# Eight pairs of row blocks by seven products in place of nine, in a feed-forward layer on one Trainium2 core

## The chip, the cores and the metric

The kernel runs on one core of a Trainium2 chip. Times are microseconds (us) of device time for one execution. The engines are named as the profile names them: PE is TensorE (matmuls; PEld its weight loads), DVE is VectorE, ACT is ScalarE, POOL is GpSimd, and SP is SyncE, which issues most of the DMA loads.

## The reference

The kernel computes a small decoder trunk: 256 tokens, 1,024 model columns (D), two layers, all in float32. Each layer is an attention (a different one per layer), a SwiGLU feed-forward of 2,816 features, and a gated embedding of 256 columns ("ple"); one RMS norm closes it. Cut to what matters here:

```python
for i in range(DEPTH):                      # 2 layers
    h = h + attention_i(rmsnorm(h))         # left out
    u = rmsnorm(h, ffn_norm_g[i])
    gu = u @ ffn_w_in[i]                    # 1024 -> 2 * 2816
    h = h + (silu(gu[..., :D_FF]) * gu[..., D_FF:]) @ ffn_w_out[i]
    gate = sigmoid(rmsnorm(h, ple_norm_g[i]) @ ple_w_gate[i])
    h = h + gate * (p[i] @ ple_w_up[i])
return rmsnorm(h, final_norm_g)
```

The change lies in the product with `ffn_w_out`, in the order of the steps around it, and in one small step of the last "ple".

## The kernel before, in words

**Numbers.** A float32 matrix is split into a high and a low part of the matmul's reduced type: ScalarE copies it (rounded) and VectorE subtracts the copy (`split`, L322 and L323, and the same inside `half`, L188 and L189, or, in pieces, L164 and L169). A product is then three matmuls, high by high, high by low and low by high (`mm3`, L100 to L102). The running sum h is held with the columns on the partitions (`hx`, printed as `gx`): eight blocks of 128 columns by 256 tokens. Its first four blocks are called half 0, the others half 1.

**Weights.** All weights lie in one array in the order of their use, 216 blocks of 128 by 1,024 values (512 KB). `half` and `blocks` take the next block: SP loads it into one of six `raw` buffers, ScalarE and VectorE split it into one of six `whi` and six `wlo` buffers. A block normally feeds 24 matmuls of 256 columns or 12 of 512. For some blocks a form is named, which splits the block in two pieces, a first block of 128 columns and the rest, or lays them apart; the constant `AGAIN` names the feature blocks, `(4, 0)` to `(20, 0)` by twos, that are split with their first eighth by itself (`_BOTH1`).

**The feed-forward (`ffn`).** The 2,816 features are 22 blocks of 128 (FT = 22), taken in eleven pairs, f = 0, 2, ... 20. For one feature block `up` makes gate and up projection, 48 matmuls into one PSUM bank (`gu`). `gated` then scales it (VectorE L631, which reads the bank), takes Silu (ScalarE L638), multiplies (VectorE L639) and splits the result into `fh` and `fl`, which are `prod[f]`. PSUM has eight banks, and each bank has one user at a time: a matmul that begins a new use waits until the old one has been read.

The product with `ffn_w_out` is made pair by pair, and its two output halves in two ways:

- Half 1 is made directly: `down(f)` takes one weight block and runs 24 matmuls (`feature_unit`) into the two banks `acc[1]` (`fo`).
- Half 0 is made for the first nine pairs (f < SEVEN = 18) by seven products in place of eight (`products`): the pair is a 2 by 2 matrix of blocks (two feature blocks by two halves of 256 output columns) times a 2 by 2 matrix (two feature blocks by two halves of 128 tokens). Seven products of three matmuls, 21, replace 24; they go into the four banks `seven` (`fs`), with tokens on the partitions. For this VectorE makes sums of the weight block (`sevenfold`, L198 to L200, `sums`) and differences of the gated features (`differences`, L651 to L653, `dif`), and both engines split the sums, the differences and the block itself.
- For the other two pairs (f = 18 and 20) half 0 is made directly, by `last(f, 0)`: 24 matmuls into `acc[0]`. `last(f, 1)` does half 1 of these pairs at the end.

**Order.** The loop at L704 runs, for each f, `up([f])`, `up([f + 1])`, then `down(f - 2)` for the pair before. At f = 16 `filler()` loads p and splits it. After `down(16)`, at f = 18, `combined` (L668) adds the four banks `fs` into a tile c: one ScalarE copy (L672, `m`) and five VectorE additions (L674 to L679). Then come `up([20])` and `up([21])`. After the loop: `last(18, 0)`; `turned(c)` (L682), which turns c back by eight transposes on TensorE (L687) into two banks `fc` and adds these to half 0 of hx (`residual`, VectorE L349, two instructions); `filler(pp)`, which is `ple_up`, the product of p with `ple_w_up` into four banks (`pu`); `last(20, 0)`; a second `residual` for half 0; `last(18, 1)`, `last(20, 1)`, and the `residual` of half 1. At `filler(pp)` four of the eight banks are held by `acc[0]` and `acc[1]`, so that `pu` needs the other four.

**Who sets the order.** A planner walks through the program ahead of the run with estimated times and fixes for each engine, and for SP's queue, one order of its instructions; it prefers what stands earlier in the program, among what its estimate says is ready. Each engine then runs its list in that order and waits where an input or a buffer isn't free. `tc.high_priority()` moves the instructions inside it ahead in the planner's preference. `tc.issue_after(x)` puts those instructions inside it that run on x's engine behind x.

**The last "ple" (layer 1).** In `ple` (L808 on), gate products in two halves are followed by the final norm. A third weight tile u (the last 256 columns of `ple_w_up`) is loaded (L871) and split (L873) into `uhi` and `ulo`; its product `pu_own` is the last work of TensorE. L868 multiplies the first half of h by the final norm's gains, one instruction for each half of the tokens (`end`). The buffers of u have the tag `qkt`, of which there are four; the split differences `dh` and `dl` of a pair take two of these.

Of the kernel before, what the change touches and what calls it, by code (L numbers as in the profile page):

```python
# [13 lines left out]
ALU = mybir.AluOpType  # L14
# [7 lines left out]
NP = H // 2  # L22
DFF = 2816
FT = DFF // P
SEVEN = FT - 4
DP = 256
EPS = 1e-6
BUCKETS = 32
# [3 lines left out]
HC = 512  # L32
# [41 lines left out]
    ((2, 8), (0, 0), 0), ((0, 0), (2, 8), 64)  # L74
FORMS = {(_l, 0, _j): _HI2 for _l in range(2) for _j in (0, 4, 6)}
FORMS.update({(_l, "wo", _n): _HI2 for _l in range(2) for _n in (0, 2, 4)})
AGAIN = tuple((f, 0) for f in range(4, FT, 2))

# [1 line left out]
def trunk(ctx: ExitStack, tc: tile.TileContext, pt, w, cst, gf, out):  # L82
    nc = tc.nc
# [6 lines left out]
    def bank(name):  # L90
        return ps.tile([P, 512], F32, tag="bank", name=name)

    def f32(ap):
        return ap.bitcast(F32)
# [3 lines left out]
    def mm3(o, a, b, start, stop):  # L98
        (ah, al), (bh, bl) = a, b
        mm(o, ah, bh, start=start, stop=False, skip_group_check=True)  # L100
        mm(o, ah, bl, start=False, stop=False, skip_group_check=True)  # L101
        return mm(o, al, bh, start=False, stop=stop, skip_group_check=True).ins  # L102
# [108 lines left out]
    def blocks(entry=False, form=None):  # L211

        if form:
            return half(APART, 0, form)
        hi, lo = half(APART, ENTRY * P if entry else 0)
        hi = [hi[:, k * P:(k + 1) * P] for k in range(KT)]
        return hi, lo if entry else [lo[:, k * P:(k + 1) * P] for k in range(KT)]
# [103 lines left out]
    def split(hi, lo, src):  # L321
        nc.scalar.activation(hi, src, AF.Copy)  # L322
        nc.vector.tensor_tensor(lo, src, f32(hi), op=ALU.subtract)  # L323
# [15 lines left out]
    def feature_unit(bks, wt, off, x, start, stop):  # L339

        hi, lo = wt
        for m in range(4):
            o = bks[m // 2][:, (m % 2) * S:(m % 2 + 1) * S]
            mm3(o, (hi[off + m], lo[off + m]), x, start and m % 2 == 0, stop)

    def residual(hf, bks):
        for b in range(2):
            at = hx[:, 4 * hf + 2 * b:4 * hf + 2 * b + 2].rearrange("p m s -> p (m s)")
            nc.vector.tensor_tensor(at, at, bks[b], op=ALU.add)  # L349
# [240 lines left out]
    def ffn(layer, nm, filler, np_):  # L590
# [3 lines left out]
        def up(fs):  # L594
# [25 lines left out]
            for a in range(2):  # L620
                wt = blocks(form=_BOTH1 if (fs[0], a) in AGAIN else None)
                for k in range(KT):
# [5 lines left out]
        def gated(fs, bks):  # L628
            for f in fs:
                t = work.tile([P, 2, S], F32, tag="t2k", bufs=3, name=f"gut{layer}_{f}")  # L630
                nc.vector.tensor_tensor(t, bks[f].rearrange("p (a s) -> p a s", s=S), nm.rows(), op=ALU.mult)  # L631
                if f >= SEVEN:
                    sg = work.tile([P, S], F32, tag="sg", name=f"sg{layer}_{f}")
# [9 lines left out]
                prod[f] = th, tl  # L643
                if f < SEVEN and f % 2:
                    differences(f // 2)

        def differences(i):

            q = quarters.pop(i).rearrange("p k (t s) -> p (k t) s", s=P)
            d = work.tile([P, 4, P], F32, tag="tt", bufs=3, name=f"dif{layer}_{i}")  # L650
            nc.vector.tensor_tensor(d[:, 0:2], q[:, 2:3].to_broadcast([P, 2, P]), q[:, 0:4:3], op=ALU.subtract)  # L651
            nc.vector.tensor_tensor(d[:, 2], q[:, 3], d[:, 0], op=ALU.subtract)
            nc.vector.tensor_tensor(d[:, 3], q[:, 1], d[:, 2], op=ALU.subtract)  # L653
            dh, dl = [work.tile([P, 4, P], F32R, tag="qkt", bufs=4, name=f"d{x}{layer}_{i}") for x in "hl"]
            split(dh, dl, d)
            diff[i] = dh, dl

        def products(i):

            b11, b22, b21, x1, x2, x3, x4 = sevenfold()  # L660
            (a11, a21), (_, a22) = [[[x[:, t * P:(t + 1) * P] for x in prod[2 * i + k]] for t in range(2)] for k in range(2)]
            a3, a7, a1, a6 = [[x[:, n] for x in diff[i]] for n in range(4)]
            m43, m1, m52, m76 = seven
            for o, at, new, a, b in ((m43, 0, 1, a22, b21), (m52, 1, 1, a21, b11), (m43, 1, 0, a3, b22), (m52, 0, 0, a11, x2),
                                     (m1, 0, 1, a1, x3), (m76, 1, 1, a6, x1), (m76, 0, 0, a7, x4)):
                mm3(o[:, at * S:(at + 1) * S], a, b, bool(new) and i == 0, i == SEVEN // 2 - 1)

        def combined():  # L668

            m43, m1, m52, m76 = [b.rearrange("p (a s) -> p a s", s=S) for b in seven]  # L670
            m = work.tile([P, 2, S], F32, tag="t2k", bufs=3, name=f"m43_{layer}")
            nc.scalar.activation(m, m43, AF.Copy)  # L672
            c = work.tile([P, 4, S], F32, tag="bias", bufs=1, name=f"c{layer}")
            nc.vector.tensor_tensor(c[:, 2], m[:, 0], m52[:, 1], op=ALU.add)  # L674
            nc.vector.tensor_tensor(c[:, 1], m[:, 1], m52[:, 0], op=ALU.add)
            o = c[:, 0:4:3]
            nc.vector.tensor_tensor(o, m, m52, op=ALU.subtract)
            nc.vector.tensor_tensor(o, o, m1[:, 0:1].to_broadcast([P, 2, S]), op=ALU.add)
            nc.vector.tensor_tensor(o, o, m76, op=ALU.add)  # L679
            return c.rearrange("p (t n) s -> p t (n s)", n=2)  # L680

        def turned(c):  # L682

            bks = [bank(f"fc{layer}_{b}") for b in range(2)]
            for m in range(4):
                for t in range(2):
                    nc.tensor.transpose(bks[m // 2][:, (m % 2) * S + t * P:(m % 2) * S + (t + 1) * P],  # L687
                                        c[:, t, m * P:(m + 1) * P], ident)
            residual(0, bks)

        def down(f):
            wt = blocks()
            for i in range(2):
                feature_unit(acc[1], wt, 4 * i, prod[f + i], f + i == 0, False)
            products(f // 2)

        def last(f, hf):

            wt = blocks(form={(FT - 2, 0): _BOTH1, (FT - 2, 1): _BOTH1}.get((f, hf)) if layer else None)
            for i in range(2):  # L700
                feature_unit(acc[hf], wt, 4 * i, prod[f + i], hf == 0 and f + i == SEVEN, f + i == FT - 1)

        early = up([0, 1])
        for f in range(2, FT, 2):  # L704
            up([f])
            up([f + 1])
            if layer == 0 and f in (6, 8, 10, 12):
                moba[0](f // 2 - 3)
            if f == FT - 6:
                pp = filler()  # L710
            if f == 2:
                seven.extend(bank(f"fs{layer}_{t}") for t in range(4))
                acc[1] = [bank(f"fo{layer}_1_{t}") for t in range(2)]
            if f < FT - 2:
                down(f - 2)
            if f == SEVEN:
                c = combined()
        acc[0] = [bank(f"fo{layer}_0_{t}") for t in range(2)]
        last(FT - 4, 0)
        turned(c)  # L720
        filler(pp)
        last(FT - 2, 0)
        residual(0, acc[0])
        last(FT - 4, 1)
        np_.turn(0)
        if layer == 0:
# [103 lines left out]
    def ple(layer, nm, ut, nx):  # L830
        if layer == 0:
            return ple_first(nm, ut, nx)
        h = token["h"]
# [8 lines left out]
        bks = [[bank(f"pg{layer}_{hf}_{t}") for t in range(2)] for hf in range(2)]  # L842
# [9 lines left out]
        gb, ys = end[:, 2], end[:, 0:2]  # L852
# [5 lines left out]
        def square(t, i, c0, c1):  # L858

            sq = work.tile([P, S], F32, tag="sg", name=f"sqf{t}_{i}") if i else \  # L860
                work.tile([P, HC], F32, tag="t2k", bufs=3, name=f"sqf{t}_{i}")
            nc.scalar.activation(sq[:, 0:c1 - c0], h[:, t, c0:c1], AF.Square, scale=D ** -0.5,
                                 accum_out=ss[:, t, i:i + 1])

        for t in range(2):
            square(t, 0, 0, HC)
            nc.vector.tensor_scalar(ms[:, t, 0:1], ss[:, t, 0:1], EPS, None, op0=ALU.add)
            nc.vector.tensor_tensor(ys[:, t, 0:HC], h[:, t, 0:HC], gb[:, 0:HC], op=ALU.mult)  # L868
        wts = [half(3 * APART) for _ in range(4)]
        uraw, uhi, ulo = [work.tile([P, 2, S], F32R if i else F32, tag="qkt", bufs=4, name=f"u{i}") for i in range(3)]  # L870
        nc.sync.dma_start(uraw, bass.AP(tensor=w.tensor, offset=w.offset + w_at(UP) + HC + S,  # L871
                                        ap=[[HW, P], [P * HW, 2], [1, S]]))
        split(uhi, ulo, uraw)  # L873
        uown = bank("pu1_own")
        own = bank(f"pg{layer}_own")

# [76 lines left out]
def _wide(a, c, hf):  # L953

    t = a[c * P:(c + 2) * P, hf * HC:(hf + 1) * HC]
    return t.reshape(2, P, HC).transpose(1, 0, 2).reshape(P, HW)


def _quarters(a, c):

    t = a[c * P:(c + 2) * P, 0:HC].reshape(2, P, 2, S)
    return np.concatenate([t[0, :, 1], t[0, :, 0], t[1, :, 1], t[1, :, 0]], 1)
# [80 lines left out]
```

## Time and profile before

| what | us |
|---|---|
| median of 3 runs | 643.4 (642.76 to 644.86) |
| the profiled execution, its own time | 641.55 |
| its span, from the first to the last instruction | 639.6 |
| TensorE busy | 630.3 (99% of the span) |
| VectorE busy | 522.6 (82%) |
| ScalarE busy | 404.9 (63%) |
| DMA traffic | 125.20 MB, mean 196 GB/s |
| granted TensorE clock | 0.998 |

The profile is one execution. A line of a group names the source line, the engine, the operation, the tile written and the tiles read (`out<-in`), the shapes, the count, then busy time, mean nanoseconds of one, and the idle time of the engine ahead of it with what ended it. A line of the timeline has the start and the length in us; a bracket at its end names idle time ahead of it and what ended that. In the list of waits stand the sum, the number of times and the longest. Matmul records have a modelled end and overlap each other: a 256-column matmul's record is 0.28 us long, though the next one starts well before that, so that the distance of starts is the better measure.

### The profile page before, as it was taken

The numbers are of one execution on the slowest core, as the hardware profiler recorded it, in microseconds if no ns is written. First come the engines' busy times: TensorE is split into PE (matmuls) and PEld (weight loads), VectorE is DVE, ScalarE is ACT, GpSimd is POOL, SyncE is SP. The second block draws the span as 40 slices with busy tenths as digits, with TensorE's granted clock in tenths as the row PEclk, the third lists the DMA queues.
The fourth block names the chain that finished last, engine by engine and source line by source line (L and its number), as shares of the span: only waits on it lengthen the run. The fifth ranks groups of instructions, "written<-read, shape, count | busy, mean of one in ns | idle before, by whom it ended". The sixth has DMA issues, their size and how long they took to land.

```text
span 639.6 us, 13330 instructions
## 1 busy us (share of the span) xinstructions
PE 630.3 (99%) x5262; PEld 608.3 (95%) x5262; DVE 522.6 (82%) x988; ACT 404.9 (63%) x737; POOL 16.3 (3%) x33
## 2 busy tenths in 40 slices
PE   9999999999999999999999999999999999999996
PEld 7899999999999999999989999999999999999885
DVE  6987985899888788889997787588988887888865
ACT  7857675766555455758875586558555555545772
POOL 2500000000000000000000000000000000000002
PEclk9999999999999999999999999999999999999999
DMA  8889744267555556776687544325666666557701
GB/s 328 303 269 372 230 152 146 78 198 230 188 191 184 182 191 205 251 232 194 201 283 246 180 150 133 132 76 188 200 198 199 198 198 198 191 200 228 239 2 66
DMA packets 37214, 125.20 MB, mean 196 GB/s; under 512 B 3968, under 2 KB 7072, under 8 KB 37152
## 3 DMA queue, kind: packets, MB, share of 16 engines
q1 hardware_dynamic: 36832, 123.91, 58.5%
q8 instruction: 41, 0.67, 0.4%
q10 hardware_dynamic: 320, 0.44, 0.2%
q14 instruction: 21, 0.17, 0.1%
HBM read 123.25 MB, written 4.24 MB: 199 GB/s over the span
## 4 chain that ended last, share of the span: by engine, by line
PE 91%; DVE 4%; issue 2%; ACT 2%; POOL 0%; POOLq 0%; DVEq 0%; ACTq 0%
PE gu L100 11%; PE gu L102 11%; PE gu L101 11%; PE pq L100 5%; PE pq L101 5%; PE pq L102 5%; PE fo L100 3%; PE fo L102 3%; PE fo L101 3%; PE wo L100 2%; PE wo L102 2%; PE wo L101 2%; PE fs L102 2%; PE fs L100 2%; PE fs L101 2%
## 5 line engine op out<-in xcount | busy, mean ns | idle before, releaser
L189 DVE TENSOR_TENSOR wlo<-raw,whi 128x1024 fp32r<-128x1024 f32 (+1 forms) x166 | 197.5, 1195 | 28.4 <-ACT whi L188 28.2
L188 ACT ACTIVATE whi<-raw 128x1024 fp32r<-128x1024 f32 (+1 forms) x166 | 169.1, 1032 | 59.1 <-issue 20.8
L100 PE MATMUL gu<-g,whi 128*128 128x256 f32 x702 | 194.0, 276 | 0.0
L102 PE MATMUL gu<-g,wlo 128*128 128x256 f32 x702 | 194.0, 276 | 0.0
L101 PE MATMUL gu<-g,whi 128*128 128x256 f32 x702 | 193.9, 276 | 0.0
L102 PEld LDWEIGHTS gu<-g,wlo 128*128 128x128 f32 x702 | 131.9, 188 | 0.0
L100 PEld LDWEIGHTS gu<-g,whi 128*128 128x128 f32 x702 | 131.8, 188 | 0.0
L101 PEld LDWEIGHTS gu<-g,whi 128*128 128x128 f32 x702 | 131.8, 188 | 0.0
L100 PE MATMUL pq<-g,whi 128*128 128x256 f32 x256 | 71.1, 278 | 0.0
L102 PE MATMUL pq<-g,wlo 128*128 128x256 f32 x256 | 70.8, 276 | 0.0
L101 PE MATMUL pq<-g,whi 128*128 128x256 f32 x256 | 70.7, 276 | 0.0
L164 ACT ACTIVATE whi<-raw 128x128 fp32r<-128x128 f32 (+1 forms) x72 | 41.8, 622 | 27.8 <-PE pq L101 6.6
L100 PE MATMUL fo<-fh,whi 128*128 128x256 f32 x208 | 57.5, 277 | 0.0
L102 PE MATMUL fo<-fh,wlo 128*128 128x256 f32 x208 | 57.5, 276 | 0.0
L101 PE MATMUL fo<-fl,whi 128*128 128x256 f32 x208 | 57.4, 276 | 0.0
L169 DVE TENSOR_TENSOR wlo<-raw,whi 128x128 fp32r<-128x128 f32 (+1 forms) x72 | 48.1, 686 | 10.4 <-ACT whi L164 10.3
L100 PEld LDWEIGHTS pq<-g,whi 128*128 128x128 f32 x256 | 48.1, 188 | 1.1 <-issue 0.7
L101 PEld LDWEIGHTS pq<-g,whi 128*128 128x128 f32 x256 | 48.1, 188 | 0.1
L102 PEld LDWEIGHTS pq<-g,wlo 128*128 128x128 f32 x256 | 48.1, 188 | 0.0
L638 ACT ACTIVATE tt<-gut 128x256 f32<-128x256 f32 x36 | 14.9, 413 | 44.1 <-DVE gut L631 44.1
L198 DVE TENSOR_TENSOR sums<-raw 128x512 f32<-128x512 f32 x18 | 12.4, 690 | 35.1 <-DMA raw<-w 35.1
L101 PEld LDWEIGHTS fo<-fl,whi 128*128 128x128 f32 x208 | 39.1, 188 | 0.0
(216 smaller groups left out, 1359.1 us busy)
## 6 DMA issues: line engine op xcount, KB each, us to landing
raw<-w SPq DMA_DIRECT2D x212, 512.0 KB, 4.2
d<-d SPq DMA_DIRECT2D x4, 768.0 KB, 9.1
raw<-w SPq DMA_DIRECT2D x8, 256.0 KB, 5.0
bias<-d SPq DMA_DIRECT2D x4, 512.0 KB, 7.8
bias<-cd SPq DMA_DIRECT2D x2, 768.0 KB, 8.1
gx<-w SPq DMA_DIRECT2D x1, 512.0 KB, 5.1
bias<-cd SPq DMA_DIRECT2D x1, 512.0 KB, 7.8
p<-pt SPq DMA_DIRECT2D x2, 256.0 KB, 4.1
```

What stands on the lines that cost most here:

```text
L100: mm(o, ah, bh, start=start, stop=False, skip_group_check=True)
L101: mm(o, ah, bl, start=False, stop=False, skip_group_check=True)
L102: return mm(o, al, bh, start=False, stop=stop, skip_group_check=True).ins
L164: nc.scalar.activation(o, raw[:, c], AF.Copy)
L169: nc.vector.tensor_tensor(t[:, a + b0 * P:a + b1 * P], raw[:, b0 * P:b1 * P], f32(ht[:, a0:a0 + (b1 - b0) * P]), op=ALU.subtract)
L188: nc.scalar.activation(hi[:, c], raw[:, c], AF.Copy)
L189: nc.vector.tensor_tensor(lo[:, c], raw[:, c], f32(hi[:, c]), op=ALU.subtract)
L198: nc.vector.tensor_tensor(more[:, 0:2], raw[:, 1:3], raw[:, 0:1].to_broadcast([P, 2, S]), op=ALU.add)
L638: nc.scalar.activation(sg, t[:, 0], AF.Silu)
```

## The change

`SEVEN` becomes FT - 6 = 16. Pair f = 16 leaves the seven products: it has no sums, differences or products, and `last(16, 0)` makes its half 0 directly, ahead of `last(18, 0)`. `combined` comes at f = 16, after `down(14)`. `turned(c)` moves from after the loop to f = 18, after `down(16)` and ahead of `up([20])`, and its `residual` gets the high priority. `AGAIN` ends at `(18, 0)`, so that the first block of `up([20])` is split in one piece. In `ple`, the split of u is placed inside `issue_after` of the second instruction of L868. The order of the weight array follows: the block of pair 16 for half 0 stands as an ordinary block behind those of `up([21])` instead of as a block of quarters.

```diff
-SEVEN = FT - 4
+SEVEN = FT - 6
-AGAIN = tuple((f, 0) for f in range(4, FT, 2))
+AGAIN = tuple((f, 0) for f in range(4, SEVEN + 4, 2))
...
         def turned(c):
-            residual(0, bks)
+            with tc.high_priority():
+                residual(0, bks)
 
         def down(f):
             wt = blocks()
             for i in range(2):
                 feature_unit(acc[1], wt, 4 * i, prod[f + i], f + i == 0, False)
-            products(f // 2)
+            if f < SEVEN:
+                products(f // 2)
 
-        def last(f, hf):
+        def last(f, hf, mid=None):
             wt = blocks(form={(FT - 2, 0): _BOTH1, (FT - 2, 1): _BOTH1}.get((f, hf)) if layer else None)
             for i in range(2):
+                if i and mid:
+                    mid()
                 feature_unit(acc[hf], wt, 4 * i, prod[f + i], hf == 0 and f + i == SEVEN, f + i == FT - 1)
...
             if f == SEVEN:
                 c = combined()
+            if f == SEVEN + 2:
+                turned(c)
         acc[0] = [bank(f"fo{layer}_0_{t}") for t in range(2)]
+        last(SEVEN, 0)
         last(FT - 4, 0)
-        turned(c)
         filler(pp)
         last(FT - 2, 0)
...
-            nc.vector.tensor_tensor(ys[:, t, 0:HC], h[:, t, 0:HC], gb[:, 0:HC], op=ALU.mult)
+            begun = nc.vector.tensor_tensor(ys[:, t, 0:HC], h[:, t, 0:HC], gb[:, 0:HC], op=ALU.mult).ins
...
-        split(uhi, ulo, uraw)
+        with tc.issue_after(begun):
+            split(uhi, ulo, uraw)
...
             if f < FT - 2:
-                seq += [_wide(fout[i], f - 2, 1), _quarters(fout[i], f - 2)]
-        seq.append(_wide(fout[i], FT - 4, 0))
+                seq += [_wide(fout[i], f - 2, 1)] + [_quarters(fout[i], f - 2)] * (f <= SEVEN)
+        seq += [_wide(fout[i], f, 0) for f in (SEVEN, FT - 4)]
```

The new parameter `mid` of `last` has no caller that uses it.

## The prediction

> **What bounds the kernel.** I read the page first: busy times, granted clock, and the engines' shares of the chain that ended last.
>
> ```profile
> PE 630.3 (99%) x5262; PEld 608.3 (95%) x5262; DVE 522.6 (82%) x988; ACT 404.9 (63%) x737; POOL 16.3 (3%) x33
> PEclk9999999999999999999999999999999999999999
> PE 91%; DVE 4%; issue 2%; ACT 2%; POOL 0%; POOLq 0%; DVEq 0%; ACTq 0%
> ```
>
> TensorE is the bound, at full clock throughout. Work taken from VectorE or ScalarE is worth nothing by itself; only fewer matmuls, or a wait of TensorE that ends, shorten the run. So the next view is the list of TensorE's waits, here in full:
>
> ```profile
> PE pu L100 <- DVE gx L349: 2.1, 2, 1.4
> PE cold L133 <- PEq L1035: 0.8, 1, 0.8
> PE pu L100 <- DVE gut L631: 0.2, 1, 0.2
> ```
>
> Apart from the start, TensorE waits only in `pu`, the filler, twice for the additions at L349 (the `residual` of `turned`) and once for the reader of a `gu` bank at L631. Matmul records overlap, so this list understates the loss. The timeline of starts shows it, layer 0 first, then layer 1:
>
> ```profile
> 284.36 0.28 PE L101 MATMUL pu<-plo,whi 128*128 128x256 f32 x1
> 284.47 0.28 PE L102 MATMUL pu<-phi,wlo 128*128 128x256 f32 x1
> 285.41 0.38 PE L100 MATMUL pu<-phi,whi 128*128 128x256 f32 x1 [0.66 <-DVE gx L349]
> 285.63 0.28 PE L101 MATMUL pu<-plo,whi 128*128 128x256 f32 x1
> ...
> 594.43 0.39 PE L101 MATMUL pu<-wlo,phi 128*128 128x512 f32 x1
> 594.66 0.40 PE L102 MATMUL pu<-whi,plo 128*128 128x512 f32 x1
> 595.25 0.50 PE L100 MATMUL pu<-whi,phi 128*128 128x512 f32 x1 [0.19 <-DVE gut L631]
> 595.58 0.40 PE L101 MATMUL pu<-wlo,phi 128*128 128x512 f32 x1
> ...
> 596.51 0.39 PE L102 MATMUL pu<-whi,plo 128*128 128x512 f32 x1
> 598.29 0.50 PE L100 MATMUL pu<-whi,phi 128*128 128x512 f32 x1 [1.39 <-DVE gx L349]
> 598.62 0.40 PE L101 MATMUL pu<-wlo,phi 128*128 128x512 f32 x1
> ```
>
> Undisturbed, starts follow each other by 0.11 us for 256 columns (284.36 to 284.47) and 0.23 for 512 (594.43 to 594.66). The first matmul after a wait also takes one extra step, so I count two steps each time. Layer 0: 284.47 to 285.63 is 1.16, less 0.22: 0.94 lost. Layer 1: 0.92 less 0.46 is 0.46, and 2.11 less 0.46 is 1.65. Together 3.05 us. Why VectorE is late shows in its own timeline, with the transposes on TensorE between:
>
> ```profile
> 284.68 1.28 DVE L349 TENSOR_TENSOR gx<-gx,fc 128x512 f32<-128x512 f32 x2
> ...
> 590.91 0.68 DVE L323 TENSOR_TENSOR u<-u,u 128x512 fp32r<-128x512 f32 x1
> 592.63 1.04 PE L687 MATMUL fc<-cs,c 128*128 128x128 f32 x8
> 594.51 0.69 DVE L631 TENSOR_TENSOR gut<-gu,row 128x512 f32<-128x512 f32 x1
> ...
> 597.55 1.28 DVE L349 TENSOR_TENSOR gx<-gx,fc 128x512 f32<-128x512 f32 x2
> ```
>
> The eight transposes end at 593.7, but VectorE still works through the last two features, weight splits and u, and adds only at 597.55. The filler needs four banks; two of them hold the transposes until these additions have read them. The bank read by L631 at 594.51 holds feature 21, and the `pu` matmul of 595.25 starts as that read ends. So the loss is one of order: VectorE's queue reaches the two additions about 4 us after their input is there.
>
> **The change, part by part.** *Ninth pair direct.* A direct half and a seven-product stage stand side by side:
>
> ```profile
> 262.21 0.28 PE L100 MATMUL fo<-fh,whi 128*128 128x256 f32 x1
> 264.93 0.28 PE L100 MATMUL fs<-whi,fh 128*128 128x256 f32 x1
> 267.35 0.28 PE L100 MATMUL gu<-g,whi 128*128 128x256 f32 x1
> ```
>
> 24 matmuls take 2.72 us, 21 take 2.42: +0.30 per layer, +0.60 in two, all on the bound engine, hidden by nothing. Bounds: two steps of 0.11 (0.44 in all) to three whole records of 0.28 (1.68); I take the measured stages, as they are the same instructions on the same tiles.
>
> [...]
>
> *What VectorE is spared.* Sums of weights, differences and their splits go, one plain split comes:
>
> ```profile
> L189 DVE TENSOR_TENSOR wlo<-raw,whi 128x1024 fp32r<-128x1024 f32 (+1 forms) x166 | 197.5, 1195 | 28.4 <-ACT whi L188 28.2
> L198 DVE TENSOR_TENSOR sums<-raw 128x512 f32<-128x512 f32 x18 | 12.4, 690 | 35.1 <-DMA raw<-w 35.1
> L323 DVE TENSOR_TENSOR wlo<-sums,whi 128x1024 fp32r<-128x1024 f32 x18 | 22.0, 1220 | 1.8 <-ACT whi L322 1.8
> ```
>
> 0.69 + 1.22 - 1.20 is at least 0.7 us per layer off VectorE, besides the smaller sums, the quarter block's split and the differences. On the end this is worth 0, since VectorE is not the bound; it is lead for what follows. The number of weight loads stays: a wide block comes where the quarter block was. Only the second raw buffer that a seven-product pair takes for its sums is no longer asked for, so SyncE's loads can run earlier, not later.
>
> *Sums a pair sooner.* `combined` (one ScalarE copy, five VectorE additions) moves ahead of `up(18)`, `up(19)` and `down(16)` in program order; the transposes move ahead of `up(20)`, `up(21)` and the direct stages. If c is not there when TensorE reaches them, everything behind them waits in TensorE's order, `up(20)` first.
>
> ```profile
> 562.84 0.28 PE L102 MATMUL fs<-whi,dl 128*128 128x256 f32 x1
> 576.58 0.28 PE L100 MATMUL fs<-whi,fh 128*128 128x256 f32 x1
> 578.88 0.28 PE L102 MATMUL fs<-whi,dl 128*128 128x256 f32 x1
> 588.38 0.68 DVE L679 TENSOR_TENSOR c<-c,fs 128x512 f32<-128x512 f32 x1
> ```
>
> Today c is finished at 589.06, 10.2 us after the last product (578.88). The transposes will stand where pair nine's products stood, 13.7 us after pair eight's (562.84 to 576.58). 3.5 us to spare, so I take 0. It can't be below nothing, as no wait for c is in the list now; upward it starts only when c slips by more than 3.5. The stretch itself has less in it than pair nine's had, by the pieces above. The eight transposes move and are not added.
>
> *Additions first.* From the transposes to `pu` lie two features and, newly, two direct stages:
>
> ```profile
> 579.00 0.28 PE L100 MATMUL gu<-g,whi 128*128 128x256 f32 x1
> 589.79 0.28 PE L102 MATMUL gu<-g,wlo 128*128 128x256 f32 x1
> ```
>
> 10.8 + 2 x 2.72 = 16.2 us for additions of 1.28, so their wait goes whole. What is late next is the bank of `up(21)`: its reader ended at 595.20, 5.4 us after the last `gu` matmul (589.79), and the two direct stages put `pu` 5.5 us after it. Even on today's timetable that just fits, and VectorE has lost c's additions and u's 0.68 from this stretch against 1.28 that come. So the 0.46 goes too.
>
> *`(20, 0)` in one piece; u later.* Rows for the lead of weights, and for u:
>
> ```profile
> 578.38 1.23 DVE L189 TENSOR_TENSOR wlo<-raw,whi 128x1024 fp32r<-128x1024 f32 x1 [0.53 <-ACT whi L188]
> 581.74 0.28 PE L100 MATMUL gu<-g,whi 128*128 128x256 f32 x1
> ...
> 573.80 0.63 ACT L322 ACTIVATE u<-u 128x512 fp32r<-128x512 f32 x1 [1.90 <-DMA u<-w]
> ...
> 627.70 0.79 DVE L839 TENSOR_TENSOR pgt<-pgt,ut 128x256 f32<-128x256 f32 x2 [2.10 <-ACT pgt L838]
> ```
>
> A block's low part is ready at 579.61 and used at 581.74: a lead of 2.1 us, the shortest near the end of the loop. The form that `(20, 0)` loses splits its first eighth ahead of the rest, so that TensorE could begin on it sooner; whole, the block is ready at most one split (1.20) later for its first matmul, inside the lead: 0. If that lead were gone, up to 0.9 per layer. Of the u split only VectorE's half is bound, behind the second addition of L868, since `issue_after` binds what runs on the engine of the instruction that it names. It then falls into the 2.10 us that VectorE stands idle before 627.70, and 0.68 fits: 0. If it lands behind 627.70 it lies on the way to the end: +0.68. Its reader, the last `pu_own` matmuls, comes later still. ScalarE's copy, with its 1.90 us wait for the load of u, stays free to come early; in before it lies ahead of pair ten's splits and costs TensorE nothing.
>
> **Sum:** -0.94 - 0.46 - 1.65 + 0.60 = -2.45 us. The profiled execution took 641.55 (span 639.6, 1.95 around it), so 639.1; on the runs' median, 643.4, it is 640.95, say 641.0, or -0.38%. The 1.85 us by which that median lies above the profiled execution I leave as it is, since nothing in the change bears on it.
>
> **The rivals.**
> *Slower: VectorE stands at the additions.* Put first in its order, they could be reached before the transposes are done. Then VectorE waits, and behind it the splits of the blocks for `up(20)` and `up(21)`, for which TensorE waits next.
>
> ```profile
> DVE sums L198 <- DMA raw<-w: 35.1, 12, 4.4
> ```
>
> VectorE does stand like that, up to 4.4 us for one load. The lead of 2.1 absorbs part; from a stand of 2.1 + 1.2 = 3.3 us per layer on, the gain is gone. A stand of 5.5 costs 3.4 per layer, 6.8 less 2.45: 647.8. Against it: VectorE runs behind TensorE here (feature 21 read 4.7 us after its matmuls), so it will come late, not early. [...]
>
> *c comes late.* `filler` loads p just ahead of pair eight's products; if ScalarE's copy of m43 goes behind the split of p and that load is late, c slips. Waiting starts at 3.5 us of slip; at 4.5 in both layers 2.0 come back: 643.0, no change.
>
> *The gu bank instead.* If VectorE reads feature 21 some 0.6 us later against TensorE than now, `pu` waits 0.5 in each layer: -1.45, 642.0, just no change. For it: 5.4 against 5.5 us is no margin by itself. Against it: what VectorE has lost from that stretch.
>
> *u's copy on ScalarE a pair sooner.* Its buffers come free a pair earlier, so its 1.90 us wait may fall among pair eight's splits; doubled, it outruns the lead by 1.7 in layer 1: -0.75, 642.7, no change.
>
> *Not what it says:* the order alone could clear the wait and the priority do nothing. Then the additions would come behind feature 21 again, but with 16.2 us instead of none between transposes and `pu` they are still in time: the forecast's 641.0, and no chance of its own.
>
> **How the numbers follow.** About 0.3% (1.9 us) is what a measurement of this kernel can tell from no change; the forecast is half a microsecond beyond it. Forecast 0.70, of which the runs' scatter and the 0.44 to 1.68 of the added matmuls put 0.13 within 0.3%; VectorE standing 0.06 (slower); c late 0.07 and u 0.07 (no change, 0.01 each slower); gu bank 0.10 (0.07 no change). That makes faster 0.60, same 0.32, slower 0.08. The range, 640.1 to 643.0, reaches below to the lower bound of the added matmuls (640.8) and the runs' scatter, above to the rivals without a change; the slower rival and the tails, some 0.15, are left out.
>
> **What would show it.** Right: no TensorE wait for gx in `pu`, starts at 0.11 and 0.23 all through it; three direct stages of 2.7 us a layer; transposes 13.7 us after the last product without a wait; u's subtraction near 625. Wrong: a `fc` matmul that waits for c, VectorE idle ahead of L349, `pu` behind gut, or `gu` behind wlo in the last pairs.

## The result, and the profile after

| | median, us | lowest to highest | ratio, with its 95% interval |
|---|---|---|---|
| before, 6 executions | 643.61 | 642.65 to 644.86 | |
| after, 6 executions | 638.66 | 638.21 to 639.21 | 0.9928 (0.9915 to 0.9940) |

The medians lie 4.95 us apart (the ratio says 0.7%), twice the 2.45 us that were forecast, and 638.66 is below the predicted range. In two later sets of runs, where the kernel before had a median of 642.4 and 642.5, the same order of instructions gained 3.5 us (e9 and e16 below). The profiled execution of after took 638.56 us, its span is 636.4.

The profile's page of after, busy times, granted clock and the shares of the chain that ended last:

```profile
PE 629.4 (99%) x5268; PEld 608.4 (96%) x5268; DVE 515.2 (81%) x968; ACT 402.7 (63%) x729; POOL 16.3 (3%) x33
PEclk9999999999999999999999999999999999999998
PE 98%; POOL 0%; issue 0%; DVE 0%; ACT 0%; POOLq 0%; DVEq 0%
```

There are six matmuls more, 7.4 us less work on VectorE, and TensorE's share of the chain rises from 91% to 98%: nothing else holds the end any more. TensorE's waits, the whole list:

```profile
PE cold L133 <- PEq L1042: 0.8, 1, 0.8
```

Only the start is left; all three waits in `pu` are gone. Its timeline around the transposes and the filler of layer 1:

```profile
575.21 0.28 PE L102 MATMUL fo<-fh,wlo 128*128 128x256 f32 x1
575.33 1.04 PE L687 MATMUL fc<-cs,c 128*128 128x128 f32 x8
...
592.42 0.28 PE L102 MATMUL fo<-fh,wlo 128*128 128x256 f32 x1
592.53 0.40 PE L100 MATMUL pu<-whi,phi 128*128 128x512 f32 x1
592.77 0.40 PE L101 MATMUL pu<-wlo,phi 128*128 128x512 f32 x1
```

The transposes start one step (0.12) after the matmul ahead of them, so they don't wait for c, and `pu` runs near its pitch of 0.23 from its first matmul. VectorE in the same stretch, with the split of u near the end:

```profile
572.68 0.68 DVE L679 TENSOR_TENSOR c<-c,fs 128x512 f32<-128x512 f32 x1
...
581.00 1.28 DVE L349 TENSOR_TENSOR gx<-gx,fc 128x512 f32<-128x512 f32 x2
...
589.17 0.68 DVE L631 TENSOR_TENSOR gut<-gu,row 128x512 f32<-128x512 f32 x1
...
622.37 0.68 DVE L323 TENSOR_TENSOR u<-u,u 128x512 fp32r<-128x512 f32 x1
624.55 0.79 DVE L845 TENSOR_TENSOR pgt<-pgt,ut 128x256 f32<-128x256 f32 x2 [1.50 <-ACT pgt L844]
```

c is complete at 573.36, 2.0 us ahead of the transposes. The additions run at 581.00, 11.5 us ahead of the filler. The bank of feature 21 is read from 589.17 on and free at 589.85, 2.7 us ahead of it. So everything on which the filler depends is there before it starts, and u's split lies in idle time, ahead of 624.55.

### The profile page after: what moved, and what is told of

Same layout as the page of the kernel before. It is cut to its first block, busy times and chain, and to the rows that moved or that the text cites. A ratio compares the mean times of both kernels' runs of the same rounds, so it can differ in the third digit from the quotient of the medians.

```text
span 636.4 us, 13306 instructions
## 1 busy us (share of the span) xinstructions
PE 629.4 (99%) x5268; PEld 608.4 (96%) x5268; DVE 515.2 (81%) x968; ACT 402.7 (63%) x729; POOL 16.3 (3%) x33
## 4 chain that ended last, share of the span: by engine, by line
PE 98%; POOL 0%; issue 0%; DVE 0%; ACT 0%; POOLq 0%; DVEq 0%
PE gu L102 13%; PE gu L101 13%; PE gu L100 13%; PE pq L100 5%; PE pq L101 5%; PE pq L102 5%; PE fo L102 4%; PE fo L101 4%; PE fo L100 4%; PE wo L100 2%; PE wo L102 2%; PE wo L101 2%; PE fs L102 2%; PE fs L101 2%; PE fs L100 2%; PE pg L101 2%
## 5 line engine op out<-in xcount | busy, mean ns | idle before, releaser
L189 DVE TENSOR_TENSOR wlo<-raw,whi 128x1024 fp32r<-128x1024 f32 (+1 forms) x170 | 202.2, 1195 | 35.3 <-ACT whi L188 35.0
L188 ACT ACTIVATE whi<-raw 128x1024 fp32r<-128x1024 f32 (+1 forms) x170 | 173.5, 1033 | 62.6 <-issue 20.8
L100 PE MATMUL fo<-fh,whi 128*128 128x256 f32 x224 | 61.9, 276 | 0.0
L102 PE MATMUL fo<-fh,wlo 128*128 128x256 f32 x224 | 61.9, 276 | 0.0
L101 PE MATMUL fo<-fl,whi 128*128 128x256 f32 x224 | 61.8, 276 | 0.0
L169 DVE TENSOR_TENSOR wlo<-raw,whi 128x128 fp32r<-128x128 f32 (+1 forms) x68 | 45.4, 686 | 12.1 <-ACT whi L164 12.1
L164 ACT ACTIVATE whi<-raw 128x128 fp32r<-128x128 f32 (+1 forms) x68 | 39.5, 622 | 23.9 <-PE pq L101 6.6
L102 PEld LDWEIGHTS fo<-fh,wlo 128*128 128x128 f32 x224 | 42.1, 188 | 0.0
L100 PEld LDWEIGHTS fo<-fh,whi 128*128 128x128 f32 x224 | 42.1, 188 | 0.0
L101 PEld LDWEIGHTS fo<-fl,whi 128*128 128x128 f32 x224 | 42.1, 188 | 0.0
```

The lines of the kernel that those rows point to most:

```text
L164: nc.scalar.activation(o, raw[:, c], AF.Copy)
L169: nc.vector.tensor_tensor(t[:, a + b0 * P:a + b1 * P], raw[:, b0 * P:b1 * P], f32(ht[:, a0:a0 + (b1 - b0) * P]), op=ALU.subtract)
L188: nc.scalar.activation(hi[:, c], raw[:, c], AF.Copy)
L189: nc.vector.tensor_tensor(lo[:, c], raw[:, c], f32(hi[:, c]), op=ALU.subtract)
```

## The experiments

Sixteen runs were made in four sets, with the kernel before run beside each set; some of them repeat a kernel. In the expectations of the first two sets, theory A is the one of the prediction (the sooner sums and additions end the waits of the filler) and B its rival (the ninth pair's work itself weighs); in the later ones V is VectorE's backlog and O the order of the additions.

### The prediction's own parts, one at a time

**e1: before, with the high priority alone.**

```diff
-            residual(0, bks)
+            with tc.high_priority():
+                residual(0, bks)
```

> Before, with only the high priority on the additions. The order of every engine comes out the same as before's, so this is also a second look at before. Theory A (the whole gain is the filler's waits, and ordinary runs of before lose more there than its profiled run's 3.05 us): time 643.6, no change, and the new profile shows about 5 us lost in pu. Theory B (before also loses in the ninth pair, where the weights' lead of 2.1 us gives out in ordinary runs): no change, about 3 us lost in pu and some 2 us in gu or fs late in the loop. Theory C (the rest is scatter of the start): no change, 3 us in pu, the rest ahead of the first layer. If the priority did the work: 641 or less.

Measured: 642.49, ratio 0.9991 (0.9970 to 1.0013): no change. The order of all engines is the one of before, instruction for instruction; the priority moves nothing.

**e2: after, with the sums and the transposes where before has them.** There are eight pairs, but `combined` comes at f = 18 and `turned(c)` just ahead of the filler. The direct block of the ninth pair still stands ahead of the filler.

```diff
-            if f == SEVEN:
-                c = combined()
             if f == SEVEN + 2:
-                turned(c)
+                c = combined()
...
+        turned(c)
         filler(pp)
```

> The changed kernel with eight pairs, but combined again at f = 18 and the transposes again just ahead of the filler, as before. Theory A: the additions come 3 to 4 us after the transposes again, the waits in pu stay, and the six added matmuls cost 0.6: 643 to 644.3. Theory B: the relief of VectorE by the ninth pair is what ordinary runs lacked: about 641.5 to 642.2.

Measured: 640.19, ratio 0.9934 (0.9918 to 0.9949), and no wait in `pu` at all. This fells theory A as I had put it: without the sooner sums and without the additions first the waits end too.

**e3: after, with ScalarE's copy of u bound late as well** (`tc.issue_after` of the square of the second half of the tokens).

> The changed kernel with ScalarE's copy of u bound late as well. It takes away ScalarE's wait of 3.34 us for the load of u, which leaves the weights a lead of 1.45 us in layer 1. Theory A: no TensorE wait hangs on it, no change against the changed kernel: 638.3 to 639.0. Theory B: some ordinary runs lose there, 638.0 to 638.4, and its scatter is smaller.

Measured: 638.55, ratio 0.9916 (0.9901 to 0.9931), as after. **e7: before, with only VectorE's split of u bound**, as the change binds it:

> Before with nine pairs and everything else in its place; only VectorE's half of the u split is bound behind L868. It takes 0.68 us from VectorE just ahead of the last features. Theory A: feature 21 and the additions come 0.68 sooner in layer 1, 0.7 to 1.2 us of the waits there go: about 643.0. If the u split carried the gain: 640 or less. If nothing hangs on it: 643.8 with the same scatter.

Measured: 642.88, ratio 1.0012 (0.9987 to 1.0037). The treatment of u carries nothing, on either engine.

**e8: seven pairs**, one more made directly than in after, its direct block inside the loop.

```diff
-SEVEN = FT - 6
+SEVEN = FT - 8
...
```

> The changed kernel taken one pair further: seven pairs by seven products, pair 14 made directly inside the loop at f = 18. With no TensorE wait left to remove, only the price of the matmuls shows. Theory A: six more matmuls, 0.30 us per layer: 639.3 against 638.7 for eight pairs. If the relief of VectorE is still worth something in some runs (Theory B): 638.7 or less. If an added direct stage is dearer than its starts show: 640 or more.

Measured: 639.26, ratio 0.9950 (0.9932 to 0.9967), no wait: 0.2 to 0.4 us above the order of after in the sets below (638.83 and 639.02), where a price of 0.30 a layer gives 0.6. These come from different sets, and the scatter doesn't allow more than that. With the waits gone, a further pair less buys nothing.

**e4: before, with the transposes behind the filler**, c in a `raw` buffer since its own is needed meanwhile.

```diff
-            c = work.tile([P, 4, S], F32, tag="bias", bufs=1, name=f"c{layer}")
+            c = work.tile([P, 4, S], F32, tag="raw", bufs=RAW, name=f"c{layer}")
...
+        filler(pp)
         turned(c)
-        filler(pp)
```

> Before with nine pairs, only the transposes moved behind the filler (c in a raw buffer, since the filler's tile takes its place). No waits of pu for the additions, and no added matmuls. Theory A: below the changed kernel by the price of six matmuls: 638.0. Theory B: before less 3.05, 640.5, since the ninth pair is still there. If the transposes then wait for ScalarE's copies of pu: up to 1 us more per layer.

Measured: 648.27, ratio 1.0063 (1.0041 to 1.0086), slower. TensorE waits for the split of the weights of `up([20])`. In layer 0 ScalarE's copy of their first piece started at 268.19 and took 0.3 us, but in VectorE's order the five additions of `combined` (from 268.32 on) now stand ahead of the split at L169, which starts only at 271.17. That c takes one of the six `raw` buffers may be why the planner chose this order; no run shows it. The longest of TensorE's waits, and the busy times by stretches (length, then busy time and count of PE, PEld, DVE, ACT and POOL, granted clock, share of the DMA engines, GB/s):

```profile
PE gu L102 <- DVE wlo L169: 5.7, 3, 2.9
```

```profile
262.00:270.10 8.10, 6.27 (x52) 5.86 (x50) 6.00 (x12) 3.96 (x8) 0.00 (x0) 1.00 0.57 204
270.10:277.00 6.90, 5.49 (x24) 5.21 (x25) 6.79 (x8) 3.32 (x5) 0.00 (x0) 0.51 0.49 162
```

So it says nothing on the order of the residual's additions: it made a new bottleneck. What it shows is that a wait can cost more than its length: during one of 2.6 us the granted clock fell, and it is 0.51 over these 6.9 us.

### How much before loses

**e5 and e6: the kernel before again**, one profile each, since its time scatters over 639 to 646 us in these sets while after's stays within 1.2.

> Before, unchanged, for another profile: its runs lie between 638.5 and 643.6 us of span, those of the changed kernel within 1. Theory A: the difference lies in pu (2.0 to 2.3 us lost in each layer where the first profile had 0.9 and 2.1). Theory B: waits of gu or fs for weights in the ninth pair or the stretch behind it. Theory D (new): a wait long enough to lower the granted clock, so that matmuls behind it start 0.23 apart in place of 0.11 for some microseconds; the clock of a run over 642 is then 0.995 or less.

> As the run above, a third profile of before, to catch an execution of another length. Each theory expects the same rows as there.

Measured: 642.45 and 645.57. The list of TensorE's waits in e6 and its stretches:

```profile
PE pu L100 <- DVE gut L631: 3.1, 2, 2.2
PE pu L100 <- DVE gx L349: 1.4, 1, 1.4
PE cold L133 <- PEq L1035: 0.8, 1, 0.8
```

```profile
282.00:286.40 4.40, 2.19 (x19) 2.00 (x18) 3.60 (x5) 2.55 (x4) 0.00 (x0) 1.00 0.73 228
286.40:289.80 3.40, 3.40 (x18) 3.29 (x17) 2.88 (x5) 2.35 (x4) 0.00 (x0) 0.50 0.73 258
289.80:300.00 10.20, 10.20 (x92) 10.20 (x92) 7.71 (x12) 7.83 (x14) 0.00 (x0) 1.00 0.47 158
```

Where the profile on which I predicted waited 0.2 us for `gut`, this one waits 3.1, and 1.3 us after the first of these waits it runs 3.4 us at half clock, which costs another 1.7. Beside the five profiles with before's order I put one number from each timeline: the **lag**, from the start of the last `gu` matmul of feature 21 to the start of L631, which reads its bank; and the excess over the pitch at the two places where `pu` stops.

| profile | lag, layer 0 / 1 | stop for `gut`, layer 0 / 1 | stop for `gx`, layer 0 / 1 | its time |
|---|---|---|---|---|
| before | 3.56 / 4.72 | none / 0.36 | 0.83 / 1.55 | 641.55 |
| e1 | 4.67 / 4.89 | 1.01 / 0.53 | 0.81 / 1.55 | 642.43 |
| e5 | 5.06 / 4.61 | 1.39 / 0.25 | 0.81 / 1.54 | 642.45 |
| e7 | 4.38 / 4.66 | 0.72 / 0.30 | 0.80 / 1.54 | 642.39 |
| e6 | 6.04 / 5.39 | 2.37 / 1.04 | (half clock) / 1.55 | 645.57 |

The pattern holds to 0.02 us. The stop for `gx` is constant, because VectorE reaches the additions a fixed time after it begins to read feature 21 (2.98 us in layer 0 and 3.04 in layer 1, in all five). The stop for `gut` is the lag less 3.66 in layer 0 and less 4.36 in layer 1 (3.56 gives none, 4.67 gives 1.01, 6.04 gives 2.37). What varies from execution to execution is VectorE's lag, and my one profile had caught it at its smallest in layer 0, just below the threshold. (e7 has before's order but for the split of u.)

### Two ways out

The next four share one set (before 642.36).

**e9: after without the priority**, the same order on all engines as after: the reference on this chip.

> The kernel after without the high priority around the additions; the order on every engine is the same as in the kernel after. It stands for the kernel after beside the three others of this set. All theories: 638.2 to 639.3 us, no wait of TensorE in pu.

Measured: 638.83 (638.48 to 639.42), ratio 0.9951 (0.9932 to 0.9970).

**e10: only the eight pairs**, that is, e2 without the binding of u as well (the high priority stays).

> Only the ninth pair of each layer is multiplied directly; the sums, the transposes, the additions and the split of u stay where the kernel before has them. Theory V (VectorE's backlog at the filler is the whole loss, and the ninth pair's VectorE work is what makes it): no wait of TensorE, and the same time as e9_after_no_priority within 0.4 us. Rival O (the earlier sums and transposes bring something of their own, of which the second experiment showed 1 to 1.5 us): 0.8 to 1.6 us above e9_after_no_priority.

Measured: 639.66, ratio 0.9956 (0.9939 to 0.9973); one execution of twelve, twice as long as all others, is left out. TensorE waits for nothing after the start. VectorE in layer 1, and TensorE's transposes there:

```profile
589.19 0.68 DVE L631 TENSOR_TENSOR gut<-gu,row 128x512 f32<-128x512 f32 x1
...
593.88 1.28 DVE L349 TENSOR_TENSOR gx<-gx,fc 128x512 f32<-128x512 f32 x2
```

```profile
591.91 1.03 PE L687 MATMUL fc<-cs,c 128*128 128x128 f32 x8
592.70 0.47 PE L100 MATMUL pu<-whi,phi 128*128 128x512 f32 x1
```

The additions start 1.2 us behind the start of the last transpose (in before 4.2), in time for the third bank of `pu`: one more direct block lies between feature 21 and the filler, and VectorE is less late (lags of 0.60 and 2.84). e10 doesn't part these two. The filler stands 2.72 us further behind feature 21 than in before, so that by the rule above the stop for `gut` would begin at lags of 6.4 and 7.1, above all of before's in the table. No wait is what theory V expected; 0.8 us above e9 is what rival O expected. These 0.8 us are not in `pu`. The landing of the last store (queue, count, KB, us from issue to landing), in after and then in e10:

```profile
out<-end ACTq DMA_DIRECT2D x1, 256.0 KB, 2.3
```

```profile
out<-end ACTq DMA_DIRECT2D x1, 256.0 KB, 3.3
```

It takes 3.3 us in the profiles of e2 and e10 and 2.3 in those of before, after, e1, e3 to e9, e11 and e12, at the very end of the span. That is about the size of the difference; why these two have it stays open. (e2 lies 1.6 us above e3, of its own set, and so shows more than this 1.0.)

**e11: nine pairs, less work for VectorE in the ninth.**

```diff
-            b11, b22, b21, x1, x2, x3, x4 = sevenfold()
+            b11, b22, b21, x1, x2, x3, x4 = sevenfold(i == SEVEN // 2 - 1)
...
+            if i == SEVEN // 2 - 1:
+                d = q
```

With the new argument `sevenfold` leaves L198 to L200 out and takes the block itself for `more`; the three differences (L651 to L653) are left out too. The ninth pair's products are then not those of the layer: the kernel is there for its time alone.

> The kernel before with nine pairs, but the ninth pair of each layer leaves out its three sums of weight blocks and its three differences of the product's blocks, and takes the blocks themselves: 1.53 + 1.00 = 2.53 us of VectorE's work less in each layer, the same matmuls in the same order. Theory V: the lag of VectorE behind feature 21 falls from 4 to 6 us to 1.5 to 3.5 us, the waits in pu from 3 to 5 us to below 1.5, and the time to 638.5 to 641, 2 to 4 us below the kernel before. Rival O (the order of the additions behind the features is the loss): the additions still stand behind two features, the waits stay at 3 us or more and the time within 1 us of the kernel before.

Measured: 638.31 (637.88 to 639.34), ratio 0.9940 (0.9919 to 0.9961). VectorE in layer 1 (lines are 3 higher), then TensorE:

```profile
590.81 0.68 DVE L634 TENSOR_TENSOR gut<-gu,row 128x512 f32<-128x512 f32 x1
...
593.86 1.28 DVE L352 TENSOR_TENSOR gx<-gx,fc 128x512 f32<-128x512 f32 x2
```

```profile
592.48 1.03 PE L693 MATMUL fc<-cs,c 128*128 128x128 f32 x8
593.28 0.47 PE L100 MATMUL pu<-whi,phi 128*128 128x512 f32 x1
593.59 0.39 PE L101 MATMUL pu<-wlo,phi 128*128 128x512 f32 x1
```

With the same matmuls in the same order as before and 2.53 us less of work on VectorE in each layer, the lag falls to 0.84 and 1.17 and `pu` never stops. This is the whole gain and, compared with e9, 0.5 more, about what the added matmuls cost. Rival O falls. The lag fell further than theory V expected (1.5 to 3.5), and e11 takes away more than work: ahead of the ninth pair's first sum VectorE stands idle for a weight load, in before's layer 1

```profile
561.08 0.69 DVE L198 TENSOR_TENSOR sums<-raw 128x512 f32<-128x512 f32 x1 [3.35 <-DMA raw<-w]
```

and for 2.7 to 3.7 us a layer in all five profiles of the table. This wait goes with the sums, and the pair's second `raw` buffer with it. So e11 shows that the ninth pair's sums and differences, with the wait ahead of them, make VectorE late; it doesn't say how much is the work and how much the wait.

**e12: after, with 3.8 us of VectorE's work put back.**

```diff
             if f < SEVEN:
                 products(f // 2)
+            else:
+                load = work.tile([P, S], F32, tag="load", bufs=1, name=f"load{layer}_{f}")
+                nc.vector.tensor_copy(load, f32(prod[f + 1][0]))
+                for _ in range(8):
+                    nc.vector.tensor_tensor(load, load, f32(prod[f + 1][0]), op=ALU.add)
```

> The kernel after with nine VectorE instructions of 128x256 more in each layer, 3.8 us, at the place where the ninth pair's work was; they compute nothing that is used. Theory V: the lag of feature 21 comes back to 3.5 to 6 us, pu waits again for the bank read at L631, 0.3 to 1.5 us a layer, and the time rises by 0.6 to 3 us over e9_after_no_priority; the additions are past by then, so less comes back than the change brought. Rival O (the earlier additions keep the filler free whatever VectorE's load): no wait, within 0.4 us of e9_after_no_priority.

Measured: 638.74, ratio 0.9951 (0.9931 to 0.9970): the time of e9, no wait. VectorE in layer 1:

```profile
585.24 1.28 DVE L349 TENSOR_TENSOR gx<-gx,fc 128x512 f32<-128x512 f32 x2
...
593.40 0.68 DVE L631 TENSOR_TENSOR gut<-gu,row 128x512 f32<-128x512 f32 x1
```

Theory V missed here. In layer 1 the lag is back at 5.75, larger than before's 4.72 (in layer 0 it is only 1.49, so that layer tests nothing), and the additions start 8.5 us behind the start of the last transpose (in after 4.9); but they still lie 8 us ahead of the filler (593.21), and the filler stands 5.55 us behind feature 21's last matmul where before had 3.63, so that by the rule above the threshold in layer 1 is 4.36 + 1.92 = 6.28. With the additions moved away and a direct block ahead of the filler, before's lag is harmless in layer 1.

### Nine pairs as a whole kernel

The last set (before 642.53) asks which way out nine pairs would have.

**e14: nine pairs, the transposes one direct block sooner**, ahead of `last(18, 0)`.

```diff
+            if f == FT - 2:
+                turned(c)
         acc[0] = [bank(f"fo{layer}_0_{t}") for t in range(2)]
         last(FT - 4, 0)
-        turned(c)
         filler(pp)
```

> The kernel before with nine pairs; only the eight transposes are issued ahead of the direct block of features 18 and 19, 2.72 us sooner, and VectorE's additions stand between the last feature's operations and not behind them. VectorE's work is unchanged. Rival O (order of the additions): the wait for gx at L349 goes, at most 0.5 us of pu's wait for the bank of feature 21 stays in each layer, 639.5 to 641. Theory V: VectorE's backlog stays 4 to 6 us, so the bank of feature 21 or the additions still make pu wait, 2 us or more; 641 to 643. Both: transposes that come ahead of c's last sums make TensorE wait at L687 by up to 2 us.

Measured: 640.17, ratio 0.9969 (0.9953 to 0.9985). TensorE's waits:

```profile
PE pu L100 <- DVE gut L631: 1.9, 2, 1.4
PE cold L133 <- PEq L1036: 0.8, 1, 0.8
```

The order alone takes the constant stop for `gx` away and no more: the lag is 5.25 and 5.06, and the stops for `gut`, 1.58 and 0.68 over the pitch, are what the rule gives for a filler 0.1 us later (1.50 and 0.60).

**e13: nine pairs, the differences of every pair on GpSimd** (`nc.gpsimd` for `nc.vector` in L651 to L653), and **e15: e13 and e14 together.**

> The kernel before with nine pairs and the whole computation; the three differences of every pair (L651 to L653) are done by GpSimd. TensorE's order stays as it was, the transposes and additions too. VectorE has 1.00 us less in each pair. Theory V (VectorE's backlog at the filler, with the additions behind it, is the loss; less work on VectorE ends it even with nine pairs): feature 21 is read 1 to 3.5 us behind its last matmul instead of 4 to 6, the waits in pu fall below 1.5 us, 638.3 to 640.5 us, which with nine pairs can come out up to 0.5 below the kernel after. Rival O (only the sooner additions, or the direct block ahead of the filler, end the waits): 3 to 5 us of waits stay, within 1 us of the kernel before. [...]

> Nine pairs, with the differences of e13 on GpSimd and the transposes of e14. If the one or the other alone ends the waits, this is no faster than the better of the two by more than 0.4 us, 638.2 to 640; if each ends a part, the parts add up.

Measured: 665.83, ratio 1.0358 (1.0337 to 1.0379), and 660.93, ratio 1.0283 (1.0262 to 1.0304). Both much slower. The two longest of TensorE's waits in e13, GpSimd's timeline for one pair, and ScalarE's next to it:

```profile
PE gu L102 <- DVE wlo L189: 13.5, 10, 2.2
PE pu L100 <- DVE gut L631: 3.7, 2, 2.4
```

```profile
213.75 0.74 POOL L651 TENSOR_TENSOR dif<-tt 128x256 f32<-128x256 f32 x1 [15.32 <-DVE tt L639]
214.57 0.52 POOL L652 TENSOR_TENSOR dif<-tt,dif 128x128 f32<-128x128 f32 x1
215.17 1.42 POOL L653 TENSOR_TENSOR dif<-tt,dif 128x128 f32<-128x128 f32 x1
```

```profile
213.96 1.04 ACT L188 ACTIVATE whi<-raw 128x1024 fp32r<-128x1024 f32 x1
216.62 0.63 ACT L322 ACTIVATE dh<-dif 128x512 fp32r<-128x512 f32 x1 [1.61 <-POOL dif L653]
217.16 1.05 ACT L188 ACTIVATE whi<-raw 128x1024 fp32r<-128x1024 f32 x1
```

The three differences take 2.84 us on GpSimd, against 1.00 on VectorE. ScalarE's queue stands at `dh` for them, 1.61 us here and 31.6 us over the 18 pairs, and the weights' copies behind it come late; VectorE's splits at L189 wait for those (35.3 us, in before 28.2), and TensorE for the splits (13.5 us). So this was no test of relief. VectorE had less to do and still ran 6 to 11 us late from feature 7 to 15, because it waited in its own order. Which way of sparing VectorE would pay in a whole kernel of nine pairs stays open.

**e16: the order of after again**, the reference of this set.

> The kernel of e9 again, the order of the kernel after on every engine, as the reference of this set: 638.3 to 639.4.

Measured: 639.02, ratio 0.9943 (0.9927 to 0.9958).

## Why the prediction was right in direction and wrong in size

**The additions (-0.94 - 1.65): right.** Their wait was constant in all five profiles with before's order (0.8 and 1.55 over the pitch), it went whole, and e14 shows what this step is worth by itself: 2.0 us (1.0 to 3.0).

**The bank of feature 21 (-0.46): the step that failed.** The mechanism was named and the arithmetic (5.4 against 5.5 us) was sound, but the term was sized from one execution. The same order of instructions stopped there for 0.36 us in that profile, 1.0 to 1.6 in e1, e5 and e7, and 3.4 with 1.7 more at half clock in e6 (both layers together, over the pitch). The prediction saw that the median lay 1.85 us above its profile and wrote "I leave as it is, since nothing in the change bears on it". As far as the profiles reach, that difference was this very wait, and the change ends it: e1, e5 and e7, all at 642.4, fit the 3.5 us of the later sets (2.6 for the additions and, with the extra steps, 1.2 to 1.9 here, less 0.6). No execution of the length of the result's median, 643.61, was profiled; it lies between these and e6. Put the other way: after, at 638.66, less the 0.6 of added matmuls, lies at 638.1, about where the profiles of before lie once their stops are taken off, each with the 0.11 of its extra step (641.55 - 3.1 = 638.5; 642.45 - 4.4 = 638.0). No other gain is needed.

**VectorE's relief ("worth nothing by itself"): wrong.** With the wait ahead of the ninth pair's sums it ends every stop by itself (e11, 4.05 us below before). Beside the change's other steps nothing of it is left to gain: with the work put back the time is that of e9 (e12). "VectorE is not the bound" is true of its share of busy time, 82%; at the filler it was the bound. It stood 3.6 to 6.0 us behind TensorE there, and the ninth pair was what kept it there.

**So there are two ways to the gain, and the change contains both.** Sparing VectorE the ninth pair's sums and differences ends the stops with the old order of the additions (e11). The earlier additions with a direct block ahead of the filler end them with VectorE's work put back (e12, layer 1). The earlier additions alone, with nine pairs, end about half (e14). A direct block ahead of the filler was never run without one of the others; e2 and e10 have it together with a less loaded VectorE.

**The added matmuls (+0.60): right, as far as the scatter lets one see.** e9 less e11 is 0.52 for one pair a layer, with ranges that overlap; e8 gives 0.2 to 0.4.

**Sums a pair sooner (0): right**, with 2.0 us to spare in place of 3.5. **Priority (no chance of its own): right**, it moves nothing. **u (0): right**: the split fell into the idle time ahead of 624.55, with 1.50 us of it left. ScalarE did take its copy of u a pair sooner, as that rival said, and its wait grew from 1.90:

```profile
557.20 0.63 ACT L322 ACTIVATE u<-u 128x512 fp32r<-128x512 f32 x1 [3.34 <-DMA u<-w]
```

TensorE did not feel it, in after, or in e3, where the copy is bound late.

**The rivals.** VectorE did not stand at the additions, c was not late, and the bank of feature 21, given 0.10 as a risk after the change, was the key to the time before it.

What is still open is why VectorE's lag differs from one execution of the same order to the next. In the five profiles of the table it is 0.31 us at feature 6, and at features 15 and 17 it lies between 5.0 and 7.5. The traces show where it grows: from feature 6 to 21 in layer 0, VectorE stood idle at L198 for weight loads for 17.2 us in the profile with the smallest lag (3.56) and for 19.6 in the one with the largest (6.04); the other three lie between in both. Whether the late loads make VectorE late, or a late VectorE frees the buffers late, no run shows.

## What to carry to other kernels

A wait that begins at a threshold (a lag less a distance) must not be sized from one execution. Work out the lag at which it starts and how far the profile stood from that; if the median of the runs lies above the profiled execution, that difference is the first candidate for the wait and not a constant to carry along. And an engine with 18% idle time can be the bound at the one place where another engine catches up with it: measure its lag there before writing its relief down as worth nothing.

## What the runs showed of the hardware

- **A wait of TensorE can cost more than its length, and its length alone doesn't say when.** In e6, layer 0, the granted clock fell to 0.50 for 3.4 us, a loss of 1.7 us, 1.3 us after a stop of 2.4 us over the pitch. In e4, layer 0, it fell 1.3 us into a stop of 2.6 us, for 6.8 us (0.51 over 6.9 us). In e13 and in e15 it fell once (mean of the execution 0.996 and 0.995), for 3.4 us, 1.5 us after stops of 2.3 and 2.0 us. After a stop of 2.55 us (e13, `pu`) and one of 3.0 us (e4, layer 1) it stayed at full speed. In the 3.4 us ahead of each of the four falls TensorE's records cover 37% to 47% of the time. Why the clock fell there and held after the two longest stops, no run shows.
- **The first matmul after a wait took longer to the next start:** 0.10 to 0.11 us more in every stop of the table at full clock, for 256 and for 512 columns (in before 0.22 us in place of 0.11 from 285.41 on, and 0.33 in place of 0.23 from 595.25 on).
- **GpSimd took 2.84 us for three small subtractions that VectorE does in 1.00** (one pair of e13). By the waits shown there, what cost the time was ScalarE's queue, which stood behind them for 31.6 us in all (in before, behind VectorE's, 5.2).
